# Layer B of a streaming encoder: four of sixteen transfers on another engine, scores and forget gates one sub-block later

## The chip, the cores and the metric

The kernel runs on one core of a Trainium2 chip. The core has a matrix engine (PE, with its weight loads PEld), a vector engine (DVE), a scalar engine (ACT), a general engine (POOL) and a queue engine (SP). Each runs its own list of instructions in order and waits on semaphores for the others. SP, ACT and POOL can issue DMA transfers. The metric is the device time of one execution in microseconds. Before the change three runs took 1830.79, 1831.72 and 1837.56 us; the median is 1831.72.

## The reference

256 frames of width 2048 pass through one layer of kind A and one of kind B, with 32 heads of 128 each. What matters here is layer B:

```python
h_kv = rms_norm(x, kv_norm)
k_s, v_s = jnp.split(h_kv @ kv_w, 2, axis=-1)
logf = jax.nn.log_sigmoid((h_kv @ f_w + f_b).astype(jnp.float32))
cum_logf_h = jnp.transpose(jnp.cumsum(logf, axis=1), (0, 2, 1))
h = rms_norm(x, b_norm[lb])
q, g = jnp.split(h @ b_w_in[lb], 2, axis=-1)
# forgetting_attention, per block of 128 queries:
sc = jnp.einsum('bqhd,bkhd->bhqk', q_b, k_b).astype(jnp.float32) * scale
decay = cum_logf_h[:, :, q0:end, None] - cum_logf_h[:, :, None, :end]
sc = jnp.where(causal[None, None], sc + decay, NEG_INF)
p = jax.nn.softmax(sc, axis=-1).astype(v.dtype)
outs.append(jnp.einsum('bhqk,bkhd->bqhd', p, v_b))
...
x = x + (o * jax.nn.silu(g)) @ b_w_out[lb]
```

All is float32.

## The kernel before

Every product is made of three matmuls: each operand is split into a high part (rounded to the engine's fast 32-bit type) and the low rest, and hi x hi, hi x lo and lo x hi are summed (`mm3`, `dot3`). The activations stay in the on-chip memory; the weights stream in. A *sub-block* is 256 rows of a 512-column unit of weights, 512 KB: SP loads it into one of three raw buffers (`bqg_raw`, `bkv_raw`), ACT makes the high part (line 233), DVE the low part (line 234), into one of four pairs of buffers, and PE uses it in twelve matmuls of 512 columns (line 177). The splits are written three sub-blocks ahead of PE.

Layer B goes through 16 groups of two heads. A group has a unit bqg (the queries and gates) and a unit bkv (keys and values) of seven sub-blocks each; the eighth of both is done together by the method of Strassen and Winograd (`products`, lines 427 to 429, the "quad"), after the third sub-block of bqg. Between the sub-blocks, the attention of the group before is advanced step by step. It is a Python generator (`side_b` with `attention`), and `drive` calls it after those sub-blocks that a table names: `B1_STEPS` for the unit bqg, `B2_STEPS` for bkv; the keys count from 0. The steps of one group's attention:

- behind bkv: the sums that make qk whole (lines 642, 648), and `turn`: DVE transposes qk in blocks of 32 (line 397) and sixteen transfers by POOL move the blocks (line 400, `b_sums<-b_quad`)
- after sub-block 2 of the next bqg: v is split (`v_split`)
- after 3: q and k are split into `wideh`, `widel`, `q1h`, `q1l` (lines 419, 420)
- after 4, two steps: the scores `s1p` and `s0p` on PE (lines 427 to 429, 451), scale and bias (458), maximum (459), exponential (461)
- after sub-block 0 of bkv: the gates are scaled into the same tile `sg` (472), and `turn` again: `sgY<-sg` on DVE, then sixteen transfers `sgZ<-sgY` of 40 KB, all by POOL
- in the next group, after its sub-blocks 0 and 1: the transposed probabilities are split (`wideh`, `widel` from `sgZ`, lines 419, 420), and the output product `op` (lines 427 to 429, 485) follows

`turn` takes a tuple `queues` of four engines; the transfers to the j-th quarter of the partitions are issued by the j-th. Layer A gives `(pool, pool, pool, act)` for its qk; everything else goes to POOL.

In group 0 the unit bkv has eight sub-blocks and carries the forget gates instead (`forget`): `zp` on PE (lines 786, 787), the transposition `fps` (794) with a chain of small DVE instructions up to `f_l` (801 to 817), the cumulative sums `cp` (828) and the transposition `cT` (834). The places are after sub-blocks 1, 2, 5 and 7.

The order on each engine is fixed when the program is built; within a step the builder may interleave instructions of different tiles.

Of the kernel before, what the change touches and what calls it, by code (L numbers as in the profile page):

```python
# [18 lines left out]
NT = S // P  # L19
# [13 lines left out]
HG = 2  # L33
# [5 lines left out]
NQ = P // SQ  # L39
# [17 lines left out]
QUAD = 7  # L57
QUAD_STEP = 3
LOAD_STEP = 5
B1_STEPS = {2: 1, 3: 1, 4: 2}  # L60
B2_STEPS = {0: 1}


def r32(ap):
    return ap.bitcast(F32)
# [3 lines left out]
def trunk(ctx, tc, x, x_t, gains, a_w_in, a_rel, a_w_out, kv_w, f_w, f_b, b_w_in, b_w_out, final_norm, out):  # L69
    nc = tc.nc  # L70
    pe, act, dve, pool, sp = nc.tensor, nc.scalar, nc.vector, nc.gpsimd, nc.sync
# [10 lines left out]
    def bank(name):  # L82
        return ps_at.tile([P, 512], F32, name=name, tag="at")
# [279 lines left out]
    def rest(u):  # L363

        for b in range(u.nk // KB - u.left, u.nk // KB):
            u.step(b)
            yield u.acc
# [24 lines left out]
    def turn(src, n, name, queues=(pool,) * NQ, home=None):  # L392

        y, z = home or [att.tile([P, NQ, n, SQ], F32, name=name + i, tag=i) for i in "YZ"]
        dve.transpose(y, src.rearrange("p n (j u) -> p j n u", u=SQ))  # L397
        for i in range(NQ):
            for j in range(NQ):
                queues[j].dma_start(out=r32(z)[j * SQ:(j + 1) * SQ, i],  # L400
                                    in_=y[i * SQ:(i + 1) * SQ, j])
        return r32(z)
# [25 lines left out]
        pe.matmul(out_, a[0], b[1], start=False, stop=False)  # L428
        pe.matmul(out_, a[1], b[0], start=False, stop=stop)  # L429

    def attention(g, biases, qk, vg, half, ocat, queues=(pool,) * NQ, line=(None, None), home=None):


        z = turn(qk.rearrange("p t (c d) -> p (t c) d", d=DH), NT * 2 * HG, "qk", queues, home)
        bias1, bias0 = biases()
        qkT = z.rearrange("p i (t c) u -> p c t i u", t=NT)
        yield
        (kh, kl), (qh, ql) = split_pairs([([qkT[:, HG + i] for i in range(HG)], "wide"),
                                          ([qkT[:, i, 1:] for i in range(HG)], "q1")], line[0])
        q0 = att.tile([P, HG, P], F32, name="q0", tag="oT")  # L440
        if line[0] is not None:
            feed.behind(q0[:, :, :1], line[0])
        act.activation(q0.rearrange("p h (i u) -> p h i u", u=SQ),
                       qkT[:, :HG, 0], AF.Copy)
        yield
        s1p = bank("s1p")[:, :].rearrange("p (i s) -> p i s", i=HG)
        s0p = bank("s0p")[:, :HG * P].rearrange("p (i s) -> p i s", i=HG)
        for i in range(HG):
            dot3(s1p[:, i], (qh[:, i], ql[:, i]), (kh[:, i], kl[:, i]))
        for i in range(HG):  # L450
            pe.matmul(s0p[:, i], q0[:, i], qkT[:, HG + i, 0], start=True, stop=True)  # L451
        NB = 1 + NT
        sg = att.tile([P, HG * NB + NT * HG, P], F32, name="sg", tag="R")
        sv = sg[:, :HG * NB].rearrange("p (i c) k -> p i (c k)", i=HG)
        nm = small.tile([P, NT, HG], F32, name="nm")
        sm = small.tile([P, NT, HG], F32, name="sm")
        for t, sp_, s_, bias in ((1, s1p, sv[:, :, P:], bias1), (0, s0p, sv[:, :, :P], bias0)):
            dve.scalar_tensor_tensor(s_, sp_, SCALE, bias, op0=OP.mult, op1=OP.add)
            dve.tensor_reduce(nm[:, t], s_, axis=AX.X, op=OP.max, negate=True)
            for i in range(HG):  # L460
                act.activation(s_[:, i], s_[:, i], AF.Exp, bias=nm[:, t, i:i + 1],
                               accum_out=sm[:, t, i:i + 1])
            if t:
                yield
        yield
        c = small.tile([P, NT, HG], F32, name="csc")
        dve.reciprocal(c, sm)
        dve.tensor_mul(c, c, half[:, :, None].to_broadcast([P, NT, HG]))
        (vh, vl, v1), gs = vg()
        for t in range(NT):  # L470
            for i in range(HG):
                act.activation(sg[:, HG * NB + t * HG + i], gs[:, t, i * DH:(i + 1) * DH], AF.Copy,
                               scale=c[:, t, i:i + 1])
        z = turn(sg, HG * NB + NT * HG, "sg")
        pT = z[:, :, :HG * NB].rearrange("p i (h c) u -> p h c i u", h=HG)
        gT = z[:, :, HG * NB:].rearrange("p i (t h) u -> p h t i u", t=NT)
        yield
        ph, pl = split([pT[:, i, :NT] for i in range(HG)], "wide", line[1])
        yield
        op = bank("op").rearrange("p (i s) -> p i s", i=HG)  # L480
        for i in range(HG):
            cols = slice(i * DH, (i + 1) * DH)
            dot3(op[:, i], (vh[:, cols], vl[:, cols]), (ph[:, i], pl[:, i]), i == 0, False)
        for i in range(HG):
            pe.matmul(op[:, i, P:], v1[:, i * DH:(i + 1) * DH], pT[:, i, NT], start=False, stop=i == HG - 1)  # L485
        yield
        oT = att.tile([P, HG, S], F32, name="oT", tag="oT")
        for i in range(HG):
            dve.tensor_mul(*(v[:, i].rearrange("p (t i u) -> p t i u", t=NT, u=SQ) for v in (oT, op)), gT[:, i])
        h0 = g * HG  # L490
        hi = ocat.hi[h0 // BIG][:, h0 % BIG:h0 % BIG + HG, :]
        lo = ocat.lo[h0 // BIG][:, h0 % BIG:h0 % BIG + HG, :]
        act.activation(hi, oT, AF.Copy)
        dve.tensor_sub(lo, oT, r32(hi))
        yield
# [186 lines left out]
    def drive(gen, side, steps, hooks={}, old=None, last=0):  # L682

        acc = None
        for i, acc in enumerate(gen):
            finish(old) if i >= last else advance(old)
            advance(side, steps.get(i, 0))
            if i in hooks:
                hooks[i]()
        return acc  # L690
# [12 lines left out]
    rs, prev, qa = [], None, quads["a"]  # L703
    for g in range(NG):
        accs = {}
        if g:
            accs["quad"] = True
            first, second = (Unit(xT, next(order)) for _ in range(2))
# [3 lines left out]
            vg = rest(second)  # L712
        else:
            first, second = woven_units()
# [3 lines left out]
        old, prev = prev, side_a(g, accs)  # L718
# [49 lines left out]
    rsB, halfB = rstd_of(tot1, "b")  # L768
# [73 lines left out]
    qb = quads["b"] = Quads(x1T, *b_tiles, lambda r, g: (b_w_in, kv_w)[r][g][QUAD], (GB, GKV))  # L842
    oB = Stat("oB", KI)

    def side_b(g, accs):
        cb = att.tile([P, HG, S], F32, name="cb", tag="tb")
        sp.dma_start(out=cb, in_=bass.AP(tensor=cumd.tensor, offset=cumd.offset + g * HG * S,
                                           ap=[[0, P], [S, HG], [1, S]]))

        def biases():  # L850
            d0 = att.tile([P, HG, P], F32, name="d0")
            for i in range(HG):
                h = g * HG + i
                act.activation(d0[:, i], cb[:, i, :P], AF.Identity, bias=cum[:, 0, h:h + 1], scale=-1.0)
                act.activation(cb[:, i], cb[:, i], AF.Identity, bias=cum[:, 1, h:h + 1], scale=-1.0)
            for ap in (cb[:, :, P:], d0):
                pool.affine_select(out=ap, in_=ap, compare_op=OP.is_ge, fill=NEG, base=0,
                                   pattern=[[0, HG], [-1, P]], channel_multiplier=1)
            return cb, d0

        qk, gs = accs["q"]
        kv = accs["kv"]
        if g:
            qb.first_half(qk[:, :, GC:], kv, NT, rsB)
            kv = qb.whole_sums(kv, NT, GC)
        else:
            evac_scaled(kv, 0, GC, rsB, qk[:, :, GC:])
        rest_of = attention(g, biases, qk, lambda: (v, gs), halfB, oB, line=(1, 2), home=qb.home)
        next(rest_of)
        yield  # L870
        v = v_split(kv, GC, rsB)
        yield
        yield from rest_of
# [11 lines left out]
    fg = forget()  # L885
    for g in range(NG):
        accs = {}
        first, second = (Unit(x1T, next(order)) for _ in range(2))
        hooks = {}
        if g:  # L890
            accs["quad"] = True
            hooks[QUAD_STEP - 1] = lambda: qb.products(first, second, (rsB, [(i, GC) for i in range(2 * NT)]))
        more = g + 1 < NG
        hooks[LOAD_STEP] = lambda: more and feed.load_quad("b", g + 1)
        accs["qg"] = drive(rest(first), prev, B1_STEPS, hooks, old, 1)
        hooks = {2: lambda: open_b(accs), 3: lambda: more and feed.differ("b")}
        accs["kv"] = drive(rest(second), prev if g else fg, B2_STEPS if g else {1: 1, 2: 1, 5: 1, 7: 1}, hooks)
        if not g:
            qb.sums_of_x()
        old, prev = prev, side_b(g, accs)  # L900
        advance(prev)
# [95 lines left out]
```

## Time and profile before

| | |
|---|---|
| runs, us | 1830.79, 1831.72, 1837.56 |
| the profiled execution, us | 1836.95 |
| its span, first to last instruction, us | 1835.2 |
| mean granted clock of PE | 0.998 |
| busy: PE, DVE, ACT, POOL, us | 1817.1, 1422.7, 1195.0, 521.0 |
| moved per second | 216 GB/s |
| layer B's groups | about 908 to 1648 us of the span |

Times in the profile are microseconds from the first instruction. A row of the timeline gives the start, the duration, the engine, the line of the kernel, the operation, the tiles as out<-in, and in brackets the idle time in front of it and what ended it. Matmuls overlap: a matmul of 512 columns shows 0.39 us, while one starts every 0.23 us.

### The profile page before, as it was taken

How to read it: one execution, taken by the hardware profiler on the slowest of the kernel's cores; microseconds unless marked ns; L12 is line 12 of the kernel's file. 1: busy time of each engine (PE TensorE's matmuls, PEld its weight loads, DVE VectorE, ACT ScalarE, POOL GpSimd, SP SyncE). 2: the span in 40 equal slices, each digit the busy share in tenths (PEclk: the TensorE clock that was granted, in tenths of full speed). 3: DMA queues.
4: the chain of work that ended last, by engine and by line, in shares of the span. 5: the costliest groups of instructions: out<-in, count | busy, mean ns of one | idle time of the engine just before them, and what ended most of it. 6: DMA issues, size and time to landing. Idle time of an engine off the chain costs nothing. (4 is left out here: it accounts for less than half of the span.)

```text
span 1835.2 us, 25999 instructions
## 1 busy us (share of the span) xinstructions
PE 1817.1 (99%) x8297; PEld 1509.0 (82%) x8297; DVE 1422.7 (78%) x2094; ACT 1195.0 (65%) x2245; POOL 521.0 (28%) x1071
## 2 busy tenths in 40 slices
PE   9999999999999999999999999999999999999998
PEld 7888888888888888888888888888888888878886
DVE  7888888887888887655578888888889988876544
ACT  6666665666666666544557777877777777765443
POOL 1333333333333333122103333333333333333000
PEclk9999999999999999999999999999999999999999
DMA  8676666666666666677756666666666666667664
GB/s 285 218 227 210 222 215 215 217 225 213 217 215 214 224 214 193 215 234 233 223 195 220 214 217 214 215 217 215 215 215 217 217 215 216 216 212 220 197 207 159
DMA packets 143146, 396.38 MB, mean 216 GB/s; under 512 B 31105, under 2 KB 37537, under 8 KB 142881
## 3 DMA queue, kind: packets, MB, share of 16 engines
q1 hardware_dynamic: 106960, 354.25, 59.6%
q0 software_dynamic: 32256, 37.29, 6.6%
q10 hardware_dynamic: 3792, 3.17, 0.6%
q8 instruction: 66, 1.08, 0.3%
q14 instruction: 72, 0.58, 0.1%
HBM read 351.05 MB, written 4.23 MB: 194 GB/s over the span
## 5 line engine op out<-in xcount | busy, mean ns | idle before, releaser
L400 POOL DMA_DIRECT2D sgZ<-sgY x512 | 250.6, 497 | 494.5 <-PE bkv_acc L177 209.0
L237 ACT ACTIVATE avg_hi<-avg_raw 128x1024 fp32r<-128x1024 f32 x112 | 118.6, 1059 | 132.9 <-DMA avg_raw<-in_a_w_in 90.0
L234 DVE SCALAR_TENSOR_TENSOR bkv_lo<-bkv_raw,gain,bkv_hi 128x512 fp32r<-128x512 f32 x226 | 159.2, 744 | 34.9 <-ACT bkv_hi L233 34.8
L234 DVE SCALAR_TENSOR_TENSOR bqg_lo<-bqg_raw,gain,bqg_hi 128x512 fp32r<-128x512 f32 x226 | 162.3, 765 | 26.5 <-ACT bqg_hi L233 25.6
L238 DVE TENSOR_TENSOR avg_lo<-avg_raw,avg_hi 128x1024 fp32r<-128x1024 f32 x112 | 136.7, 1221 | 56.1 <-ACT avg_hi L237 55.8
L233 ACT ACTIVATE bqg_hi<-bqg_raw,gain 128x512 fp32r<-128x512 f32 x226 | 150.1, 713 | 41.6 <-DMA bqg_raw<-in_b_w_in 24.3
L233 ACT ACTIVATE bkv_hi<-bkv_raw,gain 128x512 fp32r<-128x512 f32 x226 | 152.8, 713 | 37.0 <-DMA bkv_raw<-in_kv_w 19.5
L177 PE MATMUL bqg_acc<-bqg_hi,x1Th 128*128 128x512 f32 x452 | 173.5, 395 | 0.0
L177 PE MATMUL aqk_acc<-aqk_hi,xTh 128*128 128x512 f32 x452 | 172.6, 393 | 0.6 <-ACT aqk_hi L237 0.6
L177 PE MATMUL avg_acc<-avg_hi,xTh 128*128 128x512 f32 x452 | 172.3, 393 | 0.0
L177 PE MATMUL bqg_acc<-bqg_hi,x1Tl 128*128 128x512 f32 x452 | 171.8, 391 | 0.0
L177 PE MATMUL aqk_acc<-aqk_lo,xTh 128*128 128x512 f32 x452 | 170.9, 390 | 0.7 <-DVE aqk_lo L238 0.7
L177 PE MATMUL bqg_acc<-bqg_lo,x1Th 128*128 128x512 f32 x452 | 171.5, 391 | 0.0
L177 PE MATMUL aqk_acc<-aqk_hi,xTl 128*128 128x512 f32 x452 | 171.0, 390 | 0.0
L177 PE MATMUL avg_acc<-avg_hi,xTl 128*128 128x512 f32 x452 | 170.9, 390 | 0.0
L177 PE MATMUL bkv_acc<-bkv_hi,x1Th 128*128 128x512 f32 x452 | 170.9, 390 | 0.0
L177 PE MATMUL bkv_acc<-bkv_hi,x1Tl 128*128 128x512 f32 x452 | 170.7, 389 | 0.0
L177 PE MATMUL bkv_acc<-bkv_lo,x1Th 128*128 128x512 f32 x452 | 170.7, 389 | 0.0
L177 PE MATMUL avg_acc<-avg_lo,xTh 128*128 128x512 f32 x452 | 170.6, 389 | 0.0
L238 DVE TENSOR_TENSOR aqk_lo<-aqk_raw,aqk_hi 128x1024 fp32r<-128x1024 f32 x110 | 133.1, 1223 | 45.1 <-ACT aqk_hi L237 44.7
L400 POOL DMA_DIRECT2D b_sums<-b_quad x256 | 125.5, 498 | 141.9 <-DVE b_quad L397 48.2
L400 POOL DMA_DIRECT2D sums<-quad x192 | 94.2, 498 | 203.7 <-PE avg_acc L177 73.1
(318 smaller groups left out, 4377.7 us busy)
## 6 DMA issues: line engine op xcount, KB each, us to landing
bqg_raw<-in_b_w_in SPq DMA_DIRECT2D x113, 512.0 KB, 4.3
bkv_raw<-in_kv_w SPq DMA_DIRECT2D x113, 512.0 KB, 4.6
avg_raw<-in_a_w_in SPq DMA_DIRECT2D x112, 512.0 KB, 5.5
aqk_raw<-in_a_w_in SPq DMA_DIRECT2D x110, 512.0 KB, 4.2
ao_raw<-in_a_w_out SPq DMA_DIRECT2D x64, 512.0 KB, 4.3
bo_raw<-in_b_w_out SPq DMA_DIRECT2D x64, 512.0 KB, 3.9
sgZ<-sgY POOLq DMA_DIRECT2D x512, 40.0 KB, 3.9
quad<-in_a_w_in SPq DMA_DIRECT2D x32, 512.0 KB, 6.1
```

Source lines behind the costliest of these rows:

```text
L177: pe.matmul(acc[t], x[:, t * P:(t + 1) * P], w, start=t not in begun, stop=k == nk - 1 and i == 2)
L233: act.activation(hi[:, j], raw[:, j], AF.Copy, scale=gk)
L234: dve.scalar_tensor_tensor(lo[:, j], raw[:, j], gk, r32(hi[:, j]), op0=OP.mult, op1=OP.subtract)
L237: act.activation(hi[:, j], raw[:, j], AF.Copy)
L238: dve.tensor_sub(lo[:, j], raw[:, j], r32(hi[:, j]))
L400: queues[j].dma_start(out=r32(z)[j * SQ:(j + 1) * SQ, i], in_=y[i * SQ:(i + 1) * SQ, j])
```

## The change

Three edits. The scores' two steps go from behind sub-block 4 to behind sub-block 5 of bqg. `attention` gets a second tuple of queues for the transposition of `sg`, and layer B gives `(pool, pool, pool, act)`, so that four of the sixteen transfers are issued by ACT. The forget gates' middle steps go from behind sub-blocks 2 and 5 to behind 3 and 6.

```diff
-B1_STEPS = {2: 1, 3: 1, 4: 2}
+B1_STEPS = {2: 1, 3: 1, 5: 2}
...
-    def attention(g, biases, qk, vg, half, ocat, queues=(pool,) * NQ, line=(None, None), home=None):
+    def attention(g, biases, qk, vg, half, ocat, queues=(pool,) * NQ, line=(None, None), home=None, sg_queues=(pool,) * NQ):
...
-        z = turn(sg, HG * NB + NT * HG, "sg")
+        z = turn(sg, HG * NB + NT * HG, "sg", sg_queues)
...
-        rest_of = attention(g, biases, qk, lambda: (v, gs), halfB, oB, line=(1, 2), home=qb.home)
+        rest_of = attention(g, biases, qk, lambda: (v, gs), halfB, oB, line=(1, 2), home=qb.home,
+                            sg_queues=(pool, pool, pool, act))
...
-        accs["kv"] = drive(rest(second), prev if g else fg, B2_STEPS if g else {1: 1, 2: 1, 5: 1, 7: 1}, hooks)
+        accs["kv"] = drive(rest(second), prev if g else fg, B2_STEPS if g else {1: 1, 3: 1, 6: 1, 7: 1}, hooks)
```

PE, in a group in the middle of layer B, before: `bqg_hi_13860` is the fifth sub-block, `bqg_hi_13871` the sixth.

```order
L177 MATMUL bqg_acc_13753<-bqg_hi_13860,x1Tl_7097 128x512
L427 MATMUL s1p<-wideh,q1h 128x256
L428 MATMUL s1p<-widel,q1h 128x256
L451 MATMUL s0p<-b_sums,q_13928 128x128 x2
L429 MATMUL s1p<-wideh,q1l 128x256
L427 MATMUL s1p<-wideh,q1h 128x256
L177 MATMUL bqg_acc_13752<-bqg_hi_13871,x1Th_7095 128x512
L428 MATMUL s1p<-widel,q1h 128x256
L429 MATMUL s1p<-wideh,q1l 128x256
L177 MATMUL bqg_acc_13752<-bqg_lo_13872,x1Th_7095 128x512
```

The same place with the change; `bqg_hi_13894` is the seventh sub-block.

```order
L177 MATMUL bqg_acc_13753<-bqg_hi_13871,x1Tl_7097 128x512
L427 MATMUL s1p<-wideh,q1h 128x256
L428 MATMUL s1p<-widel,q1h 128x256
L429 MATMUL s1p<-wideh,q1l 128x256
L427 MATMUL s1p<-wideh,q1h 128x256
L428 MATMUL s1p<-widel,q1h 128x256
L429 MATMUL s1p<-wideh,q1l 128x256
L451 MATMUL s0p<-b_sums,q_13928 128x128 x2
L177 MATMUL bqg_acc_13752<-bqg_hi_13894,x1Th_7095 128x512
```

The scores stand twelve matmuls later, and s0p has gone behind s1p.

ACT, from the softmax of the same group on, before: the `bkv_hi` are the splits of the third to sixth kv sub-block.

```order
L461 ACTIVATE sg,sm<-sg,nm 128x256 x2
L461 ACTIVATE sg,sm<-sg,nm 128x128 x2
L233 ACTIVATE bkv_hi_13996<-bkv_raw_13900,gain 128x512
L472 ACTIVATE sg<-gs,csc 128x128 x2
L233 ACTIVATE bkv_hi_14016<-bkv_raw_13937,gain 128x512 x2
L472 ACTIVATE sg<-gs,csc 128x128 x2
L264 ACTIVATE b_quad_8504<-b_quad_8504,gain 128x512 x2
L233 ACTIVATE bkv_hi_14062<-bkv_raw_13978,gain 128x512 x2
L264 ACTIVATE b_quad_8504<-b_quad_8504,gain 128x512
L233 ACTIVATE bkv_hi_14082<-bkv_raw_14002,gain 128x512 x2
```

With the change:

```order
L461 ACTIVATE sg,sm<-sg,nm 128x256 x2
L461 ACTIVATE sg,sm<-sg,nm 128x128 x2
L264 ACTIVATE b_quad_8504<-b_quad_8504,gain 128x512
L233 ACTIVATE bkv_hi_14016<-bkv_raw_13937,gain 128x512 x2
L472 ACTIVATE sg<-gs,csc 128x128 x4
L233 ACTIVATE bkv_hi_14062<-bkv_raw_13957,gain 128x512 x2
L264 ACTIVATE b_quad_8504<-b_quad_8504,gain 128x512
L400 DMA sgZ<-sgY 32x320 x4
L233 ACTIVATE bkv_hi_14082<-bkv_raw_14002,gain 128x512 x2
L515 ACTIVATE gs<-b_comb,half_b 128x256 x2
```

The four transfers stand behind the split of the fifth kv sub-block; the four gate products stand together, and the gate's tanh (line 515) has come one split earlier.

DVE in group 0, behind the gate `gs`, as a difference:

```order
 L516 SCALAR_TENSOR_TENSOR gs<-gs,bqg_acc_8517 128x256
+L234 SCALAR_TENSOR_TENSOR bkv_lo_8788<-bkv_raw_8690,gain,bkv_hi_8787 128x512 x2
 L801 COPY f_work<-fps 128x64
 L802 TENSOR_TENSOR f_work<-f_work,fps 128x64
-L234 SCALAR_TENSOR_TENSOR bkv_lo_8814<-bkv_raw_8690,gain,bkv_hi_8813 128x512
+L234 SCALAR_TENSOR_TENSOR bkv_lo_8840<-bkv_raw_8710,gain,bkv_hi_8839 128x512
```

One split has moved in front of the first reader of `fps`.

## Rows read from the trace of the kernel before

**Rows 1.** The page: each engine's busy time in us (share of the span) and instructions.

```profile
PE 1817.1 (99%) x8297; PEld 1509.0 (82%) x8297; DVE 1422.7 (78%) x2094; ACT 1195.0 (65%) x2245; POOL 521.0 (28%) x1071
```

**Rows 2.** Waits of PE: who, for whom, us in total, times, longest.

```profile
PE s1p L429 <- DVE q1l L420: 4.2, 3, 1.9
...
PE cp L828 <- DVE f_l L817: 1.0, 1, 1.0
```

**Rows 3.** Timeline of PE at the scores: start, us, what, idle before and releaser.

```profile
1301.79 0.39 PE L429 MATMUL s1p<-wideh,q1l 128*128 128x256 f32 x1 [1.44 <-DVE q1l L420]
...
1621.98 0.39 PE L429 MATMUL s1p<-wideh,q1l 128*128 128x256 f32 x1 [1.87 <-DVE q1l L420]
```

**Rows 4.** Windows: span, busy us (count) of PE, PEld, DVE, ACT, POOL; clock; DMA; GB/s.

```profile
1296.00:1311.00 15.00, 13.56 (x65) 11.26 (x64) 12.25 (x24) 12.67 (x34) 0.00 (x0) 1.00 0.72 251
...
1615.00:1630.00 15.00, 13.13 (x56) 10.63 (x56) 11.19 (x22) 10.07 (x25) 0.00 (x0) 0.89 0.67 232
```

**Rows 5.** Timeline of SP and ACT before the last group's scores.

```profile
1611.02 0.33 SPq L904 DMA_DIRECT2D gfin<-in_final_norm  x1
...
1612.34 0.33 SPq L198 DMA_DIRECT2D bqg_raw<-in_b_w_in  x1
...
1619.55 1.33 ACT L233 ACTIVATE bqg_hi<-bqg_raw,gain 128x512 fp32r<-128x512 f32 x2 [2.52 <-DMA bqg_raw<-in_b_w_in]
```

**Rows 6.** The chain of waits: one unit of seven sub-blocks (start, us, what).

```profile
1353.27 19.04 PE bkv_acc L177 x84
```

**Rows 7.** Timeline of PE: the first quad product of four groups.

```profile
967.85 0.39 PE L427 MATMUL p<-quad_hi,x1Th 128*128 128x512 f32 x1
...
1153.14 0.39 PE L427 MATMUL p<-quad_hi,x1Th 128*128 128x512 f32 x1
...
1198.41 0.39 PE L427 MATMUL p<-quad_hi,x1Th 128*128 128x512 f32 x1
...
1608.47 0.39 PE L427 MATMUL p<-quad_hi,x1Th 128*128 128x512 f32 x1
```

**Rows 8.** Waits of ACT from 950 to 1610 us.

```profile
ACT bqg_hi L233 <- DMA bqg_raw<-in_b_w_in: 21.8, 23, 2.0
...
ACT bqg_hi L233 <- PE bkv_acc L177: 9.2, 5, 3.4
...
ACT d L854 <- DMA cb<-cumd: 9.1, 11, 1.7
...
ACT wideh L419 <- DMA sgZ<-sgY: 1.2, 1, 1.2
```

**Rows 9.** The DMA issues of line 400: duration in ns, min/median/max.

```profile
L400 POOL DMA_DIRECT2D sgZ<-sgY x512: 496/496/514, 61.7 to 1683.0; - x171
...
L400 ACTq DMA_DIRECT2D sums<-quad x64: 513/612/2180, 37.2 to 719.7; - x64
```

**Rows 10.** Timeline of DVE and PE around the output product, two groups.

```profile
1149.45 0.39 PE L428 MATMUL op<-widel,vh 128*128 128x256 f32 x1 [0.32 <-DVE widel L420]
...
1467.23 0.42 DVE L420 TENSOR_TENSOR widel<-sgZ,wideh 128x256 fp32r<-128x256 f32 x1
...
1468.92 0.28 PE L428 MATMUL op<-widel,vh 128*128 128x256 f32 x1
```

**Rows 11.** Timeline of DVE, POOL and ACT in one group, the way of the probabilities.

```profile
1447.85 1.50 DVE L397 STREAM_TRANSPOSE sgY<-sg 128x1280 f32<-128x1280 f32 x1
...
1453.24 0.70 ACT L854 ACTIVATE d<-cb,cum 128x128 f32<-128x128 f32 x2 [0.65 <-DMA cb<-cumd]
...
1458.44 1.34 ACT L233 ACTIVATE bqg_hi<-bqg_raw,gain 128x512 fp32r<-128x512 f32 x2 [0.44 <-DMA bqg_raw<-in_b_w_in]
...
1458.63 0.50 POOL L400 DMA_DIRECT2D sgZ<-sgY  x1 [0.17 <-issue]
...
1460.49 1.34 ACT L233 ACTIVATE bqg_hi<-bqg_raw,gain 128x512 fp32r<-128x512 f32 x2 [0.71 <-PE bkv_acc L177]
...
1464.62 0.73 ACT L419 ACTIVATE wideh<-sgZ 128x256 fp32r<-128x256 f32 x2
```

## The prediction

> **What bounds the kernel now.** I read the page first: the matrix engine PE is busy for 1817.1 us, 99% of the span [rows 1]. So the sum is not made of busy time but of PE's gaps, and the second view is the list of what PE waited for. In layer B it names two things that the change moves: the scores s1p waited three times for q1l, 4.2 us, and the forget gates' sums cp once for f_l, 1.0 us [rows 2]. Third, the timeline at those places: two of the three waits were 1.44 and 1.87 us [rows 3]. Fourth, the windows: around the wait of 1.87 us the granted clock is 0.89, so a part of these 15 us ran at the lower of the two levels (1.2 instead of 2.4 GHz); around the wait of 1.44 us it stays at 1.00 [rows 4]. Fifth, PE's rhythm: 84 matmuls take 19.04 us [rows 6], that is 0.227 us each and 2.72 us for a sub-block of twelve. A group that loses nothing takes 1198.41 - 1153.14 = 45.27 us; the fourteen from 967.85 to 1608.47 take 640.62 us [rows 7], 6.8 more than fourteen such. Two of the scores' waits lie in these 6.8 (4.2 - 1.9 = 2.3); the other 4.5 come mostly where the output product op needs widel, as at 1149.45, where PE sat idle for widel (0.32 us, after it had slipped in other matmuls); elsewhere widel ends 1.27 us before it is needed (1467.23 + 0.42 against 1468.92) [rows 10].
>
> **The scores, one sub-block later.** The steps that make q1l stay in the fourth sub-block, and in DVE's and ACT's order all in front of q1l stays as it was; only PE comes 2.72 us later. The longest wait is 1.87 us, so all three go: -4.2. In the last group q1l is late because it stands behind a split whose weights were issued at 1612.34, right behind the 1 MB gain gfin, and reached ACT at 1619.55 after it had waited 2.52 [rows 5]. That order is the program's, not chance, so I expect this wait in every execution. The weights are for the seventh sub-block, and PE now does the sixth before it asks for q1l. The lower clock after it (0.89 over 15 us) is worth 0.11 x 15 = 1.65 us, and goes with it.
>
> The Trainium skill's page "TensorE: Matmul & The Clock Gate" (section "HAM oscillation — how this bites in real kernels") says that a long wait for data puts the array back to half clock, so that the matmuls behind it are paid for twice. The window at 1615 agrees with that and the one at 1296 shows that not every wait does it; if the rule struck both, the term would be 3.3 instead of 1.65.
>
> What is late next: the softmax, which moves past one split on DVE and ACT and has two sub-blocks left instead of three before the transposition sgY. sgY can come 0 to 2.72 us later than at 1447.85 [rows 11]. I take 0.6, an estimate near the lower end, because in DVE's order it stands behind the same split as before (that of the fourth kv sub-block) and only has to wait for the four gate products, which ACT now does together behind that split instead of two before and two behind.
>
> **The four transfers.** POOL issues a transfer in 0.496 us, ACT one in 0.612 (0.513 to 2.180, in layer A, the only transposition where it does) [rows 9]. POOL's last issue, now at 1458.63 [rows 11], comes four issues earlier: 4 x 0.496 = 1.98, less the 0.6, so 1.4 us earlier (0.7 later at the upper end of that range). That is worth nothing by itself: ACT reads sgZ at 1464.62, and in all groups it waited there once, 1.2 us [rows 8].
>
> ACT pays 4 x 0.612 = 2.45 us in each group, placed behind the split of the fifth kv sub-block, so that sgY is ready by then and nothing stalls on it. Behind it stand ACT's splits of the last two kv and the next three bqg sub-blocks. What hides it is ACT's idle time there: 21.8 + 9.2 + 9.1 = 40.1 us over fourteen groups [rows 8], 2.9 a group. On average it just covers. But it is not spread evenly: in the group of rows 11 the idle pieces of that stretch are 0.65, 0.44 and 0.71, 1.80 together, and the third bqg split would start 2.45 - 1.80 = 0.65 us late. Between 0 (the mean) and 0.65 I take 0.45 for a group. Everything from there to op is one chain on DVE: the split's low part, the sums qk, their transposition, quad_lo, widel. So widel comes 0.45 us later. Where there is 1.27 us of slack nothing happens; in groups that lose already it is lost in full. The first four groups lose (1153.14 - 967.85) - 4 x 45.27 = 4.2 us, the ten behind them 2.6 together [rows 7]; I take eight of fourteen as without slack: 8 x 0.45 = +3.6. Bounds of this term: below, 0 (the idle time covers, or the earlier landing helps: then up to -4.5 if op's waits go); above, nothing covers, fifteen groups lose 2.45 less a mean slack of 0.6 (half of 1.27), +28. I take 3.6 because the idle row (2.9) is nearer to full cover than to none.
>
> **The forget gates.** All steps but the first and last move one sub-block. Between fps and cp still stand 39 matmuls, 39 x 0.227 = 8.85 us, as before; but DVE's order had fps's first reader right behind the layer's first gate gs, and now one split stands between the two. Of the 2.72 us by which fps comes later, what that split leaves is gained on f_l, and 1.0 is enough: -1.0; if it leaves nothing, 0. The last step follows cp after one sub-block less; the copy it needs is one short DVE instruction.
>
> **Sum.** -4.2 - 1.65 - 1.0 + 3.6 = -3.25 us. The profiled execution took 1836.95 us, 1.75 more than its span and 5.2 more than the median of 1831.72; on its own scale the change gives 1833.7. I carry the difference to the median: 1828.5.
>
> **Rivals.**
> (a) The transfers were hidden and their issue eats the gain. For it: sgZ is waited for once only. Against it: ACT's idle row. All fifteen groups lose 0.45: -6.85 + 6.75, time 1831.6. The Trainium skill speaks for this one: "DMA: Bandwidth & Descriptors" (section "Issuing engines are not separate DMA queues") holds that transfers issued by any engine run on the same DMA engines, so that spreading them saves issuing time alone. No row here contradicts it; what is saved would be POOL's 1.98 us, which nothing waits for.
> (b) Everything goes, op's waits too: the probabilities land 1.4 us earlier and the fifth kv load is now issued ahead of the quad's second half, so the late groups catch up. -6.85 - 4.5, time 1820.4; with half of op's waits 1822.6. Against it: widel is late by way of DVE's order, not of sgZ.
> (c) Slower: ACT's 2.45 us is not covered where it stands, the next group's third bqg split is late, and op waits in every group. It decides, against the gains of 6.85, from a loss of (9.2 + 6.85) / 15 = 1.07 us a group on. Fifteen groups at 1.3 to 1.85 us (the upper bound above, and some two thirds of it) are 19 to 28, less the 6.85: 1844 to 1853. For it: an ACT issue took up to 2.18 us, and half of the groups have no slack. Against it: 2.9 us idle a group. By the Trainium skill's rule on the clock (the same page and section as above) waits in each pass would cost more than their length; at the one place where the rows show this it was 1.65 us.
> (d) The scores still wait because q1l moved too: it has not in the order, so I give it no share of its own.
>
> **How the numbers follow.** The forecast has 0.50 (1825 to 1832), (a) 0.24, (b) 0.14, (c) 0.12. A measurement of this kernel can tell about 0.5% of 1831.72, 9.2 us, from no change: faster is under 1822.6, slower over 1840.9. Of (b) 0.09 lies under it, of (c) 0.11 over it; everything else is no change: 0.80. The range leaves out those two ends: 1822.5 to 1839.5.
>
> **What would show it.** Right: no wait of s1p for q1l, clock 1.00 from 1615 to 1630, no wait of cp; four issues of about 0.6 us on ACT in each group of layer B without idle time in front; POOL's last sgZ issue over 1 us earlier; groups between 45.3 and 46.5 us, with some waits of op for widel. Wrong in (c)'s way: all groups over 46.5 us, the idle time before the third bqg split gone, op waiting each time. Wrong in (b)'s way: groups of 45.3 from the first on. The forecast fails if the waits of s1p stay, or if op's grow by more than they fall.

## The result: slower by 0.3%, and the profile after

The changed kernel takes 1841.37 us, the median of 12 runs (1836.04 to 1846.59). The kernel before, beside it on the same chip, took 1834.76 (12 runs, 1830.79 to 1839.67). The ratio is 1.0032, with a 95% interval of 1.0019 to 1.0044: 5.9 us slower by the ratio (the medians are 6.6 apart), where 3.25 less were forecast. The profiled execution took 1841.45 us, its span is 1839.6.

PE's waits in the changed kernel (total us, times, longest):

```profile
PE op L428 <- DVE widel L420: 4.0, 12, 0.8
PE s1p L427 <- ACT q1h L419: 2.0, 2, 1.6
PE cp L828 <- DVE f_l L817: 0.7, 1, 0.7
```

The waits of the scores s1p for q1l are gone, 4.2 us in [rows 2]. In their place op waits for widel twelve times. One wait of s1p, 1.6 us for q1h, is new; it lies at 1667, where the last group's own scores follow, behind sums that landed late. A second trace of the same kernel (1839.61 us, run again below) has no such wait in layer B, and op waits there eight times, 2.3 us: the number of op's waits changes from execution to execution.

The window that ran at 0.89 before [rows 4] (length, busy times of PE, PEld, DVE, ACT and POOL, granted clock, DMA share, GB/s):

```profile
1615.00:1630.00 15.00, 15.00 (x73) 12.61 (x72) 12.74 (x22) 12.44 (x27) 1.38 (x3) 1.00 0.65 225
```

PE is busy throughout at full clock (2.4 GHz), and the scores that stand there, from 1627.54 on, lie inside. So the scores' part did what was forecast at its place. The loss is elsewhere, in the fourteen groups:

```profile
970.98 0.39 PE L427 MATMUL p<-quad_hi,x1Th 128*128 128x512 f32 x1
...
1614.62 0.39 PE L427 MATMUL p<-quad_hi,x1Th 128*128 128x512 f32 x1
```

They take 643.64 us, 3.0 more than in [rows 7]; ten of them are longer than the 45.27 us of a group without loss, the longest has 47.23.

This longest group is the place to look. Its first matmul starts at 1200.69. ACT (start, duration, engine, line, operation; in brackets the idle time in front and what ended it):

```profile
1222.41 1.33 ACT L233 ACTIVATE bkv_hi<-bkv_raw,gain 128x512 fp32r<-128x512 f32 x2
1223.63 0.71 ACT L264 ACTIVATE b_quad<-b_quad,gain 128x512 f32<-128x512 f32 x1
1224.08 2.44 ACTq L400 DMA_DIRECT2D sgZ<-sgY  x4
1226.64 1.34 ACT L233 ACTIVATE bkv_hi<-bkv_raw,gain 128x512 fp32r<-128x512 f32 x2 [2.30 <-DVE b_comb L648]
1227.89 0.89 ACT L515 ACTIVATE gs<-b_comb,half_b 128x256 f32<-128x256 f32 x2
1228.69 1.33 ACT L233 ACTIVATE bkv_hi<-bkv_raw,gain 128x512 fp32r<-128x512 f32 x2
...
1233.36 1.34 ACT L233 ACTIVATE bqg_hi<-bqg_raw,gain 128x512 fp32r<-128x512 f32 x2 [0.32 <-DMA bqg_raw<-in_b_w_in]
1234.61 0.89 ACT L855 ACTIVATE cb<-cb,cum 128x256 f32<-128x256 f32 x2
1236.80 1.34 ACT L233 ACTIVATE bqg_hi<-bqg_raw,gain 128x512 fp32r<-128x512 f32 x2 [1.30 <-PE bkv_acc L177]
```

The four issues take 2.44 us. The profile doesn't count issuing as busy, so it shows up as 2.30 us of idle time in front of the next split, and the bracket names a DVE instruction; but the issues end at 1226.52, and the split starts 0.12 us later. It is the sixth kv sub-block's, and it comes late by so much. The last row, the third bqg split, had waited 1.30.

DVE in the same group:

```profile
1227.40 1.41 DVE L234 SCALAR_TENSOR_TENSOR bkv_lo<-bkv_raw,gain,bkv_hi 128x512 fp32r<-128x512 f32 x2 [0.61 <-ACT bkv_hi L233]
...
1237.56 1.42 DVE L234 SCALAR_TENSOR_TENSOR bqg_lo<-bqg_raw,gain,bqg_hi 128x512 fp32r<-128x512 f32 x2 [1.66 <-ACT bqg_hi L233]
1238.89 0.48 DVE L642 SCALAR_TENSOR_TENSOR qk<-bkv_acc,rstd_b,b_comb 128x256 f32<-128x256 f32 x1
...
1242.60 0.42 DVE L420 TENSOR_TENSOR widel<-sgZ,wideh 128x256 fp32r<-128x256 f32 x1
```

DVE waits for ACT's sixth kv split, and its low part ends at 1228.81. SP's loads of the next three bqg sub-blocks:

```profile
1225.37 0.33 SPq L198 DMA_DIRECT2D bqg_raw<-in_b_w_in  x1
1228.84 0.33 SPq L198 DMA_DIRECT2D bqg_raw<-in_b_w_in  x1
1230.88 0.33 SPq L198 DMA_DIRECT2D bqg_raw<-in_b_w_in  x1
```

The second load is issued at 1228.84, right behind the end of that low part (1227.40 + 1.41): with three raw buffers, a load waits for the low part of the sub-block three before it. The third load follows in the same way the low part of the seventh (1229.43 + 1.42), 2.04 us behind the second. PE at the end of the chain:

```profile
1242.02 0.28 PE L427 MATMUL op<-wideh,vh 128*128 128x256 f32 x1
1243.07 0.39 PE L428 MATMUL op<-widel,vh 128*128 128x256 f32 x1 [0.78 <-DVE widel L420]
...
1244.01 0.39 PE L428 MATMUL op<-widel,vh 128*128 128x256 f32 x1 [0.32 <-DVE widel L420]
```

### The profile page after: what moved, and what is told of

Its sections match the earlier page's. It is cut to its first block, busy times and chain, and to the rows that moved or that the text cites. A ratio compares the mean times of both kernels' runs of the same rounds, so it can differ in the third digit from the quotient of the medians.

```text
span 1839.6 us, 26143 instructions
## 1 busy us (share of the span) xinstructions
PE 1819.6 (99%) x8297; PEld 1508.2 (82%) x8297; DVE 1419.9 (77%) x2094; ACT 1195.3 (65%) x2245; POOL 493.8 (27%) x1007
## 5 line engine op out<-in xcount | busy, mean ns | idle before, releaser
L400 POOL DMA_DIRECT2D sgZ<-sgY x448 | 219.2, 497 | 499.3 <-issue 176.9
```

The source lines that it names most:

```text
L400: queues[j].dma_start(out=r32(z)[j * SQ:(j + 1) * SQ, i], in_=y[i * SQ:(i + 1) * SQ, j])
```

## The experiments

The texts on record on blocks of copies and on tiny transfers count the kv sub-blocks from 0: their fifth is the sixth here. Ratios are to the kernel before, run beside each, with 95% intervals. "On POOL" stands for a kernel with the scores and forget gates moved and all sixteen transfers on POOL.

**The change in its parts.** All transfers on POOL:

```diff
-                            sg_queues=(pool, pool, pool, act))
+                            sg_queues=(pool, pool, pool, pool))
```

> The change with all sixteen transfers of the probabilities back on POOL; the scores behind the sixth sub-block and the forget gates one on stay. Theory 1 (the four issues on ACT cost the time, the two moves gain a little): 3 to 6 us faster than before, so 9 to 12 faster than the change; groups of 45.3 to 46 us, s1p without waits. Theory 2 (the scores' move costs the time, by a later softmax and other rows on ACT): 4 to 7 us slower than before, like the change itself. Theory 3 (the forget gates): also 4 to 7 slower.

Measured: 1830.44, ratio 0.9986 (0.9974 to 0.9998). Then the kernel before with ACT's transfers alone (of the change's diff all but the first and the last hunk):

> Before, with four of the sixteen transfers of the probabilities on ACT and nothing else. Theory 1: slower than before by more than the change is, 7 to 12 us, since the waits of s1p and the lower clock in the last group stay; op waits for widel in most groups. Theory 2: within 2 us of before. Theory 3: within 2 us of before.

Measured: 1845.70, ratio 1.0068 (1.0055 to 1.0081). The forget gates alone (the last hunk):

> Before, with only the forget gates' middle steps one sub-block later. Theories 1 and 2: within 1.5 us of before, the wait of cp about 0.7 instead of 1.0 us as in the change. Theory 3: 4 to 7 us slower, with group 1 entered late.

Measured: 1834.80, ratio 1.0002 (0.9990 to 1.0013). The scores alone, `B1_STEPS = {2: 1, 3: 1, 5: 2}`:

> Before, with only the scores behind the sixth sub-block. Theory 1: 2 to 5 us faster than before, no wait of s1p for q1l in the groups, clock 1.00 in the last group. Theory 2: 4 to 7 us slower, with op waiting for widel in most groups though ACT issues nothing.

Measured: 1830.63, ratio 0.9984 (0.9974 to 0.9993). So the scores gain 2.9 us, the forget gates nothing that can be told, and ACT's four issues cost 1.0032 - 0.9986 = 0.0046 or 8.4 us, give or take some 3. Theory 1 holds, though the first gain falls just short of its 3 to 6 us and the second loss, 12.5, goes just beyond its 7 to 12. The first kernel and the changed one differ in more than the issues: the builder also puts ACT's and DVE's instructions behind sgY in another order. The blocks of copies below show what that is worth. In the kernel on POOL, the group that stands where the longest one stood (first matmul at 1194.42) has ACT so:

```profile
1217.66 1.32 ACT L233 ACTIVATE bkv_hi<-bkv_raw,gain 128x512 fp32r<-128x512 f32 x2
...
1225.68 1.34 ACT L233 ACTIVATE bqg_hi<-bqg_raw,gain 128x512 fp32r<-128x512 f32 x2 [0.40 <-DMA bqg_raw<-in_b_w_in]
1227.83 1.34 ACT L233 ACTIVATE bqg_hi<-bqg_raw,gain 128x512 fp32r<-128x512 f32 x2 [0.81 <-PE bkv_acc L177]
```

and SP so:

```profile
1218.17 0.33 SPq L198 DMA_DIRECT2D bqg_raw<-in_b_w_in  x1
1219.89 0.33 SPq L198 DMA_DIRECT2D bqg_raw<-in_b_w_in  x1
1224.14 0.33 SPq L198 DMA_DIRECT2D bqg_raw<-in_b_w_in  x1
```

Counted from the group's first matmul, the second load is issued at 25.47 here and at 28.15 in the changed kernel, the third at 29.72 and 30.19. The third split starts at 33.41 here and at 36.11 there, 2.70 later, though its load was issued only 0.47 later. The third load takes, from issue to landing, here

```profile
DMA to landing us min/median/max: 3.6/3.6/3.6
```

and in the changed kernel, where it follows the second at 2.04 us instead of 4.25,

```profile
DMA to landing us min/median/max: 5.8/5.8/5.8
```

Either way the third split starts 0.1 us behind that landing. The bracket names PE, which frees the pair of buffers that the split writes, the sixth kv sub-block's, 33.3 us into the group in both kernels: on POOL together with the load, in the changed kernel long before it.

**Twice as many on ACT.**

```diff
-                            sg_queues=(pool, pool, pool, act))
+                            sg_queues=(pool, pool, act, act))
```

> Eight of the sixteen transfers of sgZ on ACT instead of four, the rest as in the changed kernel. Theory 1 (the time of ACT's issues delays ACT's later splits, and so the third bqg weights, widel and op): ACT pays 8 x 0.61 = 4.9 us a group and no slack is left for the second four, so the second four cost more than the first (8.4 us): 1850 to 1875 us, likeliest 1858, op waiting for widel in nearly every group. Rival (it costs something once that ACT issues at all, say its queue or the first issue, and the number is of no matter): as with four, 1837 to 1842.

Measured: 1868.39, ratio 1.0190 (1.0170 to 1.0210). PE's longest list entry:

```profile
PE op L428 <- DVE widel L420: 18.5, 15, 1.9
```

The second four cost 29 us where the first cost 8.4. The cost grows with the number, and faster than it.

**op one sub-block later.** If the loss enters PE only where op needs widel, 2.72 us more before that must take it away.

```diff
-            finish(old) if i >= last else advance(old)
+            finish(old) if i >= last else advance(old, 0 if i else 1)
...
-        accs["qg"] = drive(rest(first), prev, B1_STEPS, hooks, old, 1)
+        accs["qg"] = drive(rest(first), prev, B1_STEPS, hooks, old, 2)
```

> The changed kernel with the output product op (and what follows it) behind sub-block 2 of bqg instead of 1: PE asks for widel 2.72 us later; ACT's four issues stay. Theory 1 with its path (third bqg split, sums, quad_lo, widel, op): widel's lateness is met by the 2.72 us, and 5 to 9 of the 8.4 us come back: 1830 to 1834; op no longer waits. Rival (ACT's lateness reaches PE by other ways too, the splits of bqg above all, or the quad's matmuls that now stand in front wait in its place): less than 3 us come back, 1837 to 1842.

Measured: 1832.38, ratio 0.9996 (0.9984 to 1.0009). PE's waits:

```profile
PE s1p L429 <- DVE q1l L420: 2.2, 1, 2.2
PE s1p L427 <- ACT q1h L419: 1.9, 1, 1.9
...
PE op L428 <- DVE widel L420: 0.2, 1, 0.2
```

0.0036 or 6.6 us come back. Not all of it was the issues' cost: with all transfers on POOL the later place gains 0.0010 too (the next run). With op later the four issues still cost 0.9996 - 0.9976 = 0.0020 or 3.7 us, and by these figures 4.7 of the 8.4 enter where op needs widel. Where the rest enters is not shown; in this trace it is one group of 49.73 us, in which the scores waited for q1l. widel is as late as before or later (the second ends 42.75 us behind the group's first matmul in the mean of fourteen, 41.93 in the changed kernel), but op no longer asks before 44; thirteen of the fourteen groups take 45.1 to 45.3 us. The same with all transfers on POOL:

> All sixteen transfers on POOL, scores and forget gates as in the changed kernel, and op behind sub-block 2 of bqg instead of 1. By theory 1 what is left of op's waits goes: the fourteen groups take 636.1 us where fourteen without loss would take 633.5, so up to 2.6 us: 1827.5 to 1830. Rival (op's evacuation and the split of v now come between the quad's parts and the next sub-blocks' splits, and something there is late): 1831 to 1836.

Measured: 1828.80, ratio 0.9976 (0.9965 to 0.9987): faster than the kernel before by 0.24% and than the changed kernel by 0.56%, the fastest of all here.

**The same four on SP.**

```diff
-                            sg_queues=(pool, pool, pool, act))
+                            sg_queues=(pool, pool, pool, sp))
```

> The four transfers that the changed kernel gives to ACT are issued by SP, whose other work is to issue the loads; all else as in the changed kernel. If ACT's time is the cost and POOL's relief is worth nothing: as all on POOL, 1829 to 1833. Rival (SP runs its list in order, too: its four issues wait for sgY and hold up the weights' loads behind them, so that raw weights come late): 1836 to 1845. If fewer issues on POOL were worth something: under 1828.

Measured: 1850.43, ratio 1.0095 (1.0077 to 1.0114). The rival held, and cost more than its 1836 to 1845. SP's rows in one group:

```profile
1226.84 2.41 SPq L400 DMA_DIRECT2D sgZ<-sgY  x4
1229.36 0.99 SPq L198 DMA_DIRECT2D bqg_raw<-in_b_w_in  x2
1230.40 0.68 SPq L847 DMA_DIRECT2D cb<-cumd  x1
```

The first two bqg loads stand behind the four issues and go out together, and ACT waits for the first:

```profile
1233.20 1.34 ACT L233 ACTIVATE bqg_hi<-bqg_raw,gain 128x512 fp32r<-128x512 f32 x2 [1.65 <-DMA bqg_raw<-in_b_w_in]
```

**ACT's time, or the transfers?** In these kernels all sixteen transfers are on POOL, and ACT does something else in the place of its four issues, on data that nobody reads. First four copies, which the builder put one by one in front of the halves of the next two splits:

```diff
+        queues[-1] or [act.activation(src[:, :4].rearrange("p n (j u) -> p j n u", u=SQ), y[:, :, :4], AF.Copy) for _ in range(NQ)]
```

> All sixteen transfers on POOL, and at the place of ACT's four issues four copies on ACT of 128x512 from sgY into the dead tile sg, which nobody reads: 4 x 0.63 = 2.5 us of ACT's time for each group, without a transfer. Theory 1 (it is ACT's time, whatever fills it): as the changed kernel, 1837 to 1842, op's waits for widel 3 to 5 us. Rival (ACT's queue of transfers, or what these do beside the weights, costs the time): as the kernel with all on POOL, 1829 to 1832.

Measured: 1833.89, ratio 1.0006 (0.9992 to 1.0020). Between the two theories. Eight copies in one block, `act.activation(src[:, i], y[:, :, i], AF.Copy)` for i from 0 to 7:

> All sixteen transfers on POOL; at the place of ACT's four issues eight copies on ACT of 128x128 from sgY into separate parts of the dead tile sg: 8 x 0.294 = 2.35 us in one block in front of both halves of the fifth kv sub-block's split. The four copies before stood each in front of one half of a split, so that the first half lost 0.6 us only. Theory A (ACT's time as a block is the whole cost): as the changed kernel, 1837 to 1842. Rival B (ACT's time is worth what the four copies cost, 1834, and the rest comes from issuing transfers): 1833 to 1836.

Measured: 1835.63, ratio 1.0007 (0.9993 to 1.0021). By the figures rival B, but the block held ACT for 1.5 us only, so it decides little. Four tiny transfers on ACT, `act.dma_start(out=src[:SQ, i, :1], in_=y[:SQ, i, 0, :1])`:

> All sixteen transfers of sgZ on POOL; at the place of ACT's four issues ACT issues four transfers of 32x1 elements from sgY into the dead tile sg, which nobody reads. Theory A (what costs is the time for which ACT is held by four issues in front of the split of the fifth kv sub-block, whatever they move): as the changed kernel, 1837 to 1842, with issues of about 0.6 us. Rival B (what the 40 KB transfers do in ACT's queue, or that POOL has four fewer, costs a part): nearer to the kernel with copies or to all on POOL, 1829 to 1835.

Measured: 1886.69, ratio 1.0285 (1.0265 to 1.0305). Neither theory, and the experiment was badly built. DVE:

```profile
1151.28 0.88 DVE L642 SCALAR_TENSOR_TENSOR qk<-bqg_acc,rstd_b,b_comb 128x256 f32<-128x256 f32 x2 [1.19 <-DMA sg<-sgY]
```

qk takes over sg's buffer, so DVE stood until the tiny transfer had landed, and the low parts behind it came late. The next kernels write into a tile of their own (`junk`, in the buffer of `oT`). Those with transfers have the changed kernel's order on ACT and DVE throughout; with eleven and thirteen copies DVE's is the same and on ACT `d` (line 854) has moved behind a bqg split; with seventeen copies some sums of qk have changed places on DVE as well. Eleven copies:

```diff
+        junk = None if queues[-1] else att.tile([P, HG, S], F32, name="junk", tag="oT").rearrange("p a (b k) -> p (a b) k", k=P); queues[-1] or [act.activation(junk[:, i % 4], y[:, :, i % 8], AF.Copy) for i in range(11)]
```

> All sixteen transfers on POOL; at the place of ACT's four issues eleven copies of 128x128 from sgY into a tile of its own that nobody reads or waits for. One copy of such a block took 0.21 us after the one before, so 11 x 0.21 = 2.3 us, the time by which the four issues held up ACT (2.30); the block of eight before was 1.5 us only and held the tile that the sums qk need. Theory A (ACT's time is the whole cost): as the changed kernel, 1837 to 1842. Rival B (ACT's time is under half of the cost, and the rest comes with the transfers): 1832 to 1836.

Measured: 1835.89, ratio 0.9997 (0.9983 to 1.0010): by the figures rival B again. Tiny transfers into `junk`:

> All sixteen transfers on POOL; at the place of ACT's four issues ACT issues four transfers of 32x1 elements from sgY into the tile that nobody waits for, so that the sums qk don't wait for their landing, as they did when the target was sg. Theory A (the time for which ACT is held): 2.3 us as in the changed kernel, 1837 to 1842. Rival B (it is the 40 KB that each of ACT's transfers moves, or POOL's four fewer): 1832 to 1836. Rival C (any issue by ACT slows more than its own 0.6 us, whatever lands): as far out as with the target sg, over 1860.

Measured: 1840.57, ratio 1.0025 (1.0007 to 1.0042). Full ones of 40 KB into `junk`, beside POOL's sixteen:

> All sixteen transfers on POOL, and besides at the place of ACT's four issues four transfers by ACT of 40 KB each, 32x320 elements from sgY into the tile that nobody waits for: ACT's time and its transfers without POOL's four fewer. Theory A (ACT's time alone): as the changed kernel, 1837 to 1842. Rival D (the 160 KB a group that now move beside the weights cost too): 1843 or more. Rival E (that POOL has four fewer is what costs, for instance because the transfers land in another order): 1832 to 1836.

Measured: 1841.46, ratio 1.0036 (1.0022 to 1.0050). 0.1 KB or 40 KB, and whether POOL has four fewer or not, cost the same within the intervals. But the copies seemed to be cheaper than issues, although DVE's order was the changed kernel's: that order alone doesn't cost the 8.4 us. ACT with the eleven:

```profile
1219.62 2.30 ACT L402 ACTIVATE junk<-sgY 128x128 f32<-128x128 f32 x11
1221.82 1.32 ACT L233 ACTIVATE bkv_hi<-bkv_raw,gain 128x512 fp32r<-128x512 f32 x2
```

The copies overlap with the split behind them by 0.1 us; behind the issues it started 0.12 us later. Over fourteen groups the next split starts 2.40 us behind sgY's end with eleven copies, and 2.67 with the four issues. So thirteen and seventeen copies, and the changed kernel again:

> As the kernel with the block of eleven copies, with thirteen: 13 x 0.21 = 2.7 us of ACT's time. The split of the fifth kv sub-block began 2.40 us behind the transposition sgY with eleven copies and 2.67 with the four issues of the changed kernel, so here at 2.8. Theory A (ACT's time is the whole cost, of which the first 1.5 us were hidden and the rest is paid): 1839 to 1845, ratio to the kernel before 1.003 to 1.006. Rival B (issuing a transfer costs something beside ACT's time): 1834 to 1838, ratio under 1.0020.

> The same with seventeen copies, 3.5 us of ACT's time, the split at 3.65 us behind sgY. Theory A: paid nearly in full from the changed kernel's 2.67 on, (3.65 - 2.67) x 15 = 14.7 us more than it, of which eight on ACT showed three quarters: 1848 to 1856. Rival B: half of that, 1841 to 1847.

> The changed kernel itself, as the yardstick of the two blocks of copies on the same chip and beside the same runs of the kernel before: ratio 1.0032 as in its first timing, within 0.0018 of it, 1837 to 1842 by either theory.

Measured: thirteen 1841.30, ratio 1.0040 (1.0026 to 1.0053); seventeen 1852.73, ratio 1.0091 (1.0074 to 1.0108); the changed kernel 1839.95, ratio 1.0029 (1.0016 to 1.0041). Theory A holds within the noise: ACT's time costs, whatever fills it. The kernels together (means over the fourteen groups of one trace each; the last four columns in us from the group's first matmul; cost is the ratio less 0.9986, times 1833, with some 3 us either way):

| in the place of the issues | split behind sgY's end | second load | third load (to landing) | third bqg split | second widel's end | cost, us |
|---|---|---|---|---|---|---|
| nothing (on POOL) | 0.86 | 26.30 | 30.16 (3.64) | 33.95 | 41.34 | 0 |
| eleven copies | 2.40 | 27.61 | 29.64 (4.79) | 34.57 | 41.73 | 2.0 |
| four issues (the change) | 2.67 | 27.94 | 29.96 (4.56) | 34.75 | 41.93 | 8.4, 7.9 |
| thirteen copies | 2.85 | 28.25 | 30.27 (4.74) | 35.15 | 42.30 | 9.9 |
| seventeen copies | 3.60 | 29.17 | 31.19 (4.90) | 36.20 | 43.36 | 19.3 |
| eight issues | 5.23 | 30.44 | 32.47 (3.92) | 36.54 | 43.90 | 37.4 |

## Why the prediction was wrong

**The step that failed** is "What hides it is ACT's idle time there ... 2.9 a group. On average it just covers", and with it the term of +3.6. Measured, the four issues cost 8.4 us, 0.56 in each of fifteen groups. The idle time was used up; in the changed kernel the rows of ACT between 968 and 1610 are

```profile
L233 ACT ACTIVATE bqg_hi<-bqg_raw,gain 128x512 fp32r<-128x512 f32 x196 | 130.2, 713 | 10.0 <-DMA bqg_raw<-in_b_w_in 6.4 <-DVE bqg_lo L234 1.6 <-PE bkv_acc L177 1.3
L854 ACT ACTIVATE d<-cb,cum 128x128 f32<-128x128 f32 x30 | 10.2, 387 | 0.5 <-DMA cb<-cumd 0.5
```

and in the kernel on POOL, over its fourteen groups,

```profile
L233 ACT ACTIVATE bqg_hi<-bqg_raw,gain 128x512 fp32r<-128x512 f32 x196 | 130.2, 713 | 20.1 <-DMA bqg_raw<-in_b_w_in 15.2 <-PE bkv_acc L177 4.7
L854 ACT ACTIVATE d<-cb,cum 128x128 f32<-128x128 f32 x28 | 11.0, 394 | 7.6 <-DMA cb<-cumd 7.5
```

10.5 and 27.7 us of idle time, where the prediction had 40.1. Its rows begin at 950, and 35.3 of the 40.1 lie in the fourteen groups, 2.5 a group; with the scores moved they are 2.0 a group, less than the 2.45 that four issues take. And idle time in front of the bqg splits is not all spare time: ACT waits there mostly for weights, and the second load is issued when the low part of the sixth kv sub-block is done, which stands behind ACT's own split of it. Make ACT late there and the load goes out late: 1.6 us in the mean (27.94 against 26.30). It then runs 2.0 instead of 3.9 us ahead of the third, which takes 4.56 instead of 3.64 us to land. (The distance alone doesn't make it 4.56: with eight issues it is 2.0 too, and the third takes 3.92. In all rows of the table the third lands 2.5 to 3.2 us behind the second, and the second lands late.) So the third bqg split comes 0.80 late and the second widel 0.59, and op needs it 41.8 us into the group, as in the kernel on POOL (first matmul at 1194.42), where nothing waits:

```profile
1236.22 0.28 PE L428 MATMUL op<-widel,vh 128*128 128x256 f32 x1
```

The mean passes from 41.34, in time, to 41.93, late. That ACT's time costs, and how much, is shown by the blocks of copies, and that by the figures over half of it enters at op, by the kernels with op later; the steps over the loads between are read from the traces, and no run changes them alone. From eleven to seventeen copies each further us costs (19.3 - 2.0) / (3.60 - 2.40) = 14.4 us, nearly all of fifteen groups. By that line, an estimate from two kernels, the cost begins at 2.40 - 2.0/14.4 = 2.26, 1.4 us behind the 0.86 without a block: so much was hidden, not 2.9. The line gives 5.9 us for the changed kernel's 2.67, and 8.4 and 7.9 were measured, which the intervals (about 0.0013 or 2.4 us either way) allow; a share of some 2 us for the transfers themselves isn't excluded. Of the term's two factors, 0.45 us a group was near the 0.59 by which widel came late. Counting eight groups as without slack was the second error: ten of the fourteen are longer than 45.27 us in the changed kernel, and the longest groups of the profile of before were not the only ones at the edge.

**The scores: mechanism right, size off.** The order, the waits that go and the clock at 1615 came as forecast. But the edit alone gives 2.9 us (0.0007 to 0.0026 of the time, 1.3 to 4.8), not 5.85. In its profile the waits for q1l are gone and op's are 1.4 us, so the gain was not turned into them. The sum took its terms from one execution, of 1836.95 us, 2 to 4 us above the medians measured since. The kernel with the forget gates alone, whose scores stay where they were, tells the two terms apart: the waits come again, 4.2 us in all and 1.62 in the last group, as the prediction expected of every execution,

```profile
1618.70 0.39 PE L429 MATMUL s1p<-wideh,q1l 128*128 128x256 f32 x1 [1.62 <-DVE q1l L420]
```

but the clock behind them doesn't fall:

```profile
1609.00:1624.00 15.00, 13.38 (x65) 10.99 (x64) 12.80 (x26) 11.80 (x32) 0.00 (x0) 1.00 0.73 260
```

So the -1.65 for the clock is not there in every execution, and -4.2 alone lies within the measured interval. Together with ACT's issues the move is worth more: without it those alone cost 0.0068, with it the kernel is at 1.0032.

**The forget gates.** -1.0 was forecast; cp waits 0.7 instead of 1.0 in the changed kernel's first trace and 0.2 in its second and with the forget gates alone. Alone the edit gives 1.0002 (0.9990 to 1.0013), in which 0.8 us can't be told from nothing.

**What was right about the transfers.** Four issues of 0.61 us; POOL's last issue 1.5 us earlier (it ends 31.18 us into the group in the mean, 32.7 before; 1.4 was forecast), and that was worth nothing that can be told: with four transfers more on POOL the cost was the same.

**The rivals.** (a), all groups lose 0.45, was nearest to the truth with 6.75 us; it failed on the gains. (c) had the right place, op waiting for widel, and a price, 19 to 28 us, that four issues don't come near. (b) fell: the late groups didn't catch up. The measured time lies between (a), 1831.6, and (c), 1844 and more, where no rival stood, because the way over the loads was not looked at. 1839.5 as the upper end isn't worked out either; the end that the text names is 1840.9. And 3.0 of the 12.9 us between 1828.5 and 1841.37 are the base: 1831.72 was the median of three runs, and that of twelve is 1834.76.

The Trainium skill's rule named for (a) ("DMA: Bandwidth & Descriptors", section "Issuing engines are not separate DMA queues") agrees with the runs: 0.1 and 40 KB cost the same within the intervals, and what was paid is mainly the time that it takes to initiate the transfers. It adds that this time is usually small relative to the transfer. Here 0.61 us stands against 4.5 to landing, which agrees, and yet the issue decided.

## What to carry to other kernels

Idle time of an in-order engine is safe cover only if what it waits for doesn't depend on its own earlier work; follow the wait back through the buffers before counting it. A moved transfer costs the issuing engine its issue time in a block, and the profile shows that block as idle. Where one late value has a fixed moment of use, as op has, moving the use (6.6 us here, 1.8 of them without the issues on ACT too) can be worth more than hurrying the value.

## What the runs showed of the hardware

A transfer of 0.1 KB on ACT's queue took 3.9 us (median) to land in the two kernels with tiny transfers, one of 40 KB 4.5 in the changed kernel and 4.9 beside POOL's sixteen. The first of the two:

```profile
sg<-sgY ACTq DMA_DIRECT2D x64, 0.1 KB, 3.9
```

Beside four transfers of 40 KB on ACT's queue a load lands later. The first bqg load, issued 24 to 25 us into the group, takes 5.4 us to land in the mean of the changed kernel's groups, 5.5 in its second trace and beside POOL's sixteen, but 4.3 on POOL and 4.5 with eleven copies or with tiny transfers. That this costs time is not shown.

After the wait of 2.15 us for q1l in the kernel with op later, PE's matmuls started every 0.43 instead of 0.23 us; the granted clock of the next 4.5 us and of those behind them (columns as above) was

```profile
1164.00:1168.50 4.50, 4.46 (x15) 3.54 (x15) 4.50 (x9) 3.40 (x8) 0.00 (x0) 0.62 0.75 242
1168.50:1173.00 4.50, 4.50 (x22) 3.67 (x21) 3.04 (x6) 4.44 (x15) 0.00 (x0) 1.00 0.93 354
```

That group took 49.73 us where its neighbours took 45.25: it lost 4.48 us for a wait of 2.15. This agrees with the rule of the Trainium skill that the prediction named (the page "TensorE: Matmul & The Clock Gate", section "HAM oscillation — how this bites in real kernels"): after a long wait the array is back at half clock, and the work behind it is paid for twice. Not every wait does it. A wait of 1.63 us for q1h in the changed kernel, at 1667, was followed by no lower clock:

```profile
1655.00:1685.00 30.00, 28.37 (x132) 23.33 (x132) 18.34 (x27) 14.96 (x32) 12.30 (x26) 1.00 0.64 201
```
